# Second mixer of a two-layer backbone: queries and output projection with both parts of the rows side by side, two products a chunk for three

## The chip, the cores and the metric

The kernel is one program on one core of a Trainium2 chip. The metric is the device time of one execution in microseconds, the median of several runs. Five engines work side by side: TensorE (PE in the profile, with its weight loads as PEld), VectorE (DVE), ScalarE (ACT), GpSimd (POOL) and SyncE (SP), which issues nearly all DMA transfers. Each engine takes its own instructions strictly in an order that is fixed when the program is built; between engines there are semaphores only.

## The reference, cut to what matters

There are two layers over 256 latent and 256 context tokens of width 1024. The second layer's mixer is grouped-query attention, and since it is the last layer only the latent tokens get queries and an output:

```python
def odd_mixer(h_lat, h_ctx, w_in, w_out, qg, kg, cos, sin, need_ctx_out):
    q, k, v = split_cols(h_lat @ w_in, SIZES_ODD)           # 8 heads of 128; 2 key/value heads
    q = apply_rope(rms_norm(q.reshape(B, S, H_C, HD_C), qg), cos, sin) * HD_C ** -0.5
    k = apply_rope(rms_norm(k.reshape(B, S, KV_C, HD_C), kg), cos, sin)
    ...
    ck, cv = split_cols(h_ctx @ w_in[:, H_C * HD_C:], SIZES_ODD[1:])
    ...
    out_lat = block_attention(q, k_all, v_all) @ w_out
# in the layer loop
x_lat = x_lat + g1 * o_lat
h_lat = modulate(x_lat, norm_ffn_g[l], sh2, sc2)
y_lat = moe(h_lat, router_w, router_b, exp_w1[l], exp_w3[l], exp_w2[l])
```

## The kernel before, in words

Rows are kept transposed, features on the 128 partitions and tokens along the free axis (context in columns 0 to 255, latent tokens in 256 to 511). A projection by a 32-bit weight W of rows X is made on TensorE in a faster 32-bit format of fewer bits, so both operands are split into a high part and what is left of it, the low part: W = hi + lo, X = xhi + xlo. One chunk (128 of the 1024 input features) is then three products into the same accumulator, hi·xhi, lo·xhi and hi·xlo, made by `mm3` (line 1356; the products stand in the profile under line 1358). Weights are split by `splitw` (ScalarE casts hi at line 286, VectorE subtracts to get lo at line 287; two buffers of each).

The second mixer begins at line 1761 and goes through these stages, given by the order in which the code at its end issues them. An engine's instructions are put in order when the program is built, and products of neighbouring stages are mixed where the earlier ones would wait.

- `normed(m)` (lines 1784 to 1787) makes the high and the low part of the normalised rows, for latent tokens (m = 1) and then for context tokens (m = 0), for each of 8 chunks j: VectorE multiplies, ScalarE writes `h_hi[j]`, GpSimd makes the full value, VectorE subtracts to write `h_lo[j]`. These are the tiles g_hi and g_lo of the trace.
- `heads` (line 1821) with `head` (1798) makes the queries of heads 0 to 3 and the keys of the two key heads; later, between the attention of heads 0 to 3, the queries of heads 4 to 7. A head of queries is 8 chunks of three products over 256 columns; a head of keys is over all 512. `head` then squares the accumulator on ScalarE (1805) and scales it on VectorE into q1 or k1 (1806). `turn` (1809), issued one head later, sums the squares on TensorE (1812), rotates (1815 to 1819).
- `values` makes v; it and the keys are not touched by the change.
- `attend(h)` (1866 to 1889): scores (1871), softmax (1875 to 1879), transposes (1882, 1883), product with v (1886); ScalarE writes the high part of the result, `o_hi[h]` (1888), VectorE the low part `o_lo` (1889). `o_hi` takes over the buffers of q1.
- `out_half1(k0)` (1893) is the output projection, in two halves of four heads (k0 = 0 and 4); each makes 8 groups of 128 output features (2 weight tiles, m = 0 to 3 in each), a group being 4 chunks of three products over 256 columns. Then `residual` (1680, VectorE, 1684) adds gate times the accumulator to the residual stream XT. The first half is mixed with the attention of heads 4 to 7 and with products for the conditioning vectors (`bg`, line 261). The second half is mixed with `step(j)` of the expert front: square on ScalarE (341), scaling on VectorE (348), sums on TensorE (235).
- After it come the router and the experts of layer 1, whose weights stream through a ring of 1 MB buffers; a transfer is issued when a product has freed a buffer.

PSUM accumulators have tags with few buffers: "a", "t" and "o" have two each, "pj" and "ad" one.

Of the kernel before, what the change touches and what calls it, by code (L numbers as in the profile page):

```python
# [16 lines left out]
P = 128  # L17
# [66 lines left out]
def _model(tc, nc, ctx, A, out, dbg):  # L84
# [9 lines left out]
    def pt_(shape, tag, dt=F32):  # L94

        return psum.tile(shape, dt, tag=tag, name=tag, bufs=PB[tag])
# [1677 lines left out]
    A1, B1 = affine(1, 0, "mix")  # L1774
    h_hi = [hp.tile([P, T], F32R, name=f"g_hi{j}") for j in range(J)]
    h_lo = [hp.tile([P, T], F32R, name=f"g_lo{j}") for j in range(J)]

# [11 lines left out]

    q1 = [c1.tile([P, S], F32, tag="q1", name="q1", bufs=H_C) for _ in range(H_C)]  # L1790
    k1 = c1.tile([P, KV_C, T], F32, name="k1")
    v1 = c1.tile([P, NB, KV_C * HD_C], F32, name="v1")
    o_hi = {}
    o_lo = c1.tile([P, H_C, S], F32R, name="o_lo")
    rq1 = c1.tile([P, H_C, 2], F32, name="rq1")
    rk1 = c1.tile([P, KV_C, NB], F32, name="rk1")

    def head(hi, lo, dst, g, t0, tag):

        n = T - t0  # L1800
        ps = pt_([P, n], tag)
        for k in range(J):
            mm3(ps, hi[:, k, :], lo[:, k, :], h_hi[k][:, t0:], h_lo[k][:, t0:], k == 0, k == J - 1)
        sq = wt_([P, T], "y")[:, 0:n]
        SC.activation(sq, ps, AF.Square)
        V.tensor_scalar(dst, ps, g, None, op0=OP.mult)
        return sq
# [58 lines left out]
    def attend(h):  # L1866
# [18 lines left out]
        for c in range(NB):  # L1885
            PE.matmul(o, lhsT=v1[:, c, kv * P:(kv + 1) * P], rhs=pT[:, c, :], start=(c == 0), stop=(c == NB - 1))  # L1886
        o_hi[h] = c1.tile([P, S], F32R, tag="q1", name="o_hi", bufs=H_C)
        SC.copy(o_hi[h], o)
        V.tensor_tensor(o_lo[:, h, :], o, o_hi[h].bitcast(F32), op=OP.subtract)

    w_out1 = A["odd_w_out"][0].rearrange("(j p) c -> p j c", p=P)

    def out_half1(k0):
        for c in range(2):
            w = wtile(w_out1[:, k0:k0 + 4, c * 512:(c + 1) * 512], 4, 512)
            for m in range(4):
                hi, lo = splitw(w[:, :, m * P:(m + 1) * P])
                ps = pt_([P, S], ("pj", "o")[m % 2] if k0 else "pj")
                for k in range(4):
                    mm3(ps, hi[:, k, :], lo[:, k, :], o_hi[k0 + k], o_lo[:, k0 + k, :], k == 0, k == 3)  # L1900
                residual(c * 4 + m, ps, 2, 1, 1)
                yield
# [125 lines left out]
```

## Time and profile before

| | us |
|---|---|
| median of 3 runs | 1099.69 (1099.27 to 1100.06) |
| profiled execution, its own time | 1100.19 |
| span from its first to its last instruction | 1098.3 |
| TensorE busy | 984.2 (90%) |
| VectorE busy | 559.7 (51%) |
| ScalarE busy | 399.6 (36%) |

The second mixer lies at about 690 to 844 us of the span. In the profile L1358 is line 1358 of the kernel; a row of a group gives the busy time, the mean length of one and the idle time of the engine before it with what ended it. A timeline row gives start, length, engine, line, operation, output and inputs, shapes, and in brackets the idle time before and its releaser. Matmuls are pipelined: the start of one is recorded, its end is modelled, so the price of one in a stream is read from start to start.

### The profile page before, as it was taken

What the parts mean: (1) busy time and instruction counts of PE and PEld (TensorE: products, weight loads), DVE (VectorE), ACT (ScalarE), POOL (GpSimd) and SP (SyncE); (2) the same over time, 40 slices, a digit from 0 to 9 for tenths busy, and PEclk for the clock granted to TensorE, in tenths of its full rate; (3) what the DMA queues carried; (4) which work ended last, traced back from release to release, by engine and by line L of the source; (5) the groups of instructions that cost most, each with busy time, mean ns of one, the idle gap of its engine ahead of it and who ended that gap; (6) DMA issues with size and microseconds to landing.
All of it is one profiled execution on the core that took longest, in us unless ns stands there. A gap on an engine that the chain in (4) does not pass through costs nothing.

```text
span 1098.3 us, 14558 instructions
## 1 busy us (share of the span) xinstructions
PE 984.2 (90%) x5327; PEld 616.7 (56%) x5327; DVE 559.7 (51%) x1333; ACT 399.6 (36%) x735; POOL 91.1 (8%) x87
## 2 busy tenths in 40 slices
PE   5799999999999559999899999799998899988865
PEld 1577845556776357565566545468766454433322
DVE  3543389645877659575465623745766621101101
ACT  2532254437445227464535533324344121111100
POOL 0300000002000301211120100410100100000000
PEclk9899999999999769999989999899999799999988
DMA  9932237492328519999999999560198599999993
GB/s 376 300 123 83 77 146 256 168 340 77 123 109 322 215 56 361 388 392 395 401 404 383 409 401 371 201 232 2 61 357 348 205 419 420 420 419 420 421 419 113
DMA packets 71580, 305.70 MB, mean 278 GB/s; under 512 B 6096, under 2 KB 27856, under 8 KB 41168
## 3 DMA queue, kind: packets, MB, share of 16 engines
q1 hardware_dynamic: 61904, 290.23, 66.8%
q0 software_dynamic: 3072, 11.01, 3.8%
q10 hardware_dynamic: 6528, 3.47, 1.1%
q8 instruction: 44, 0.72, 0.3%
q14 instruction: 32, 0.26, 0.1%
HBM read 293.16 MB, written 11.53 MB: 277 GB/s over the span
## 4 chain that ended last, share of the span: by engine, by line
PE 30%; DMA 14%; DVE 4%; ACT 1%; issue 1%; POOL 0%; SPq 0%; DVEq 0%; ACTq 0%; POOLq 0%
DMA w<-in_exp_w_dram 13%; PE o L1011 5%; PE pj L1358 4%; PE o L235 3%; PE o L1050 2%; PE o L1886 1%; PE t L1358 1%; PE pj L998 1%; PE a L1871 1%; PE a L261 1%; PE o L1358 1%; DVE lo L287 1%; DMA xg<-rows,idx 1%; PE ad L261 1%; PE t L1882 1%; PE t L681 1%
## 5 line engine op out<-in xcount | busy, mean ns | idle before, releaser
L287 DVE TENSOR_TENSOR lo<-w,hi 128x1024 fp32r<-128x1024 f32 (+2 forms) x170 | 179.6, 1077 | 52.2 <-ACT hi L286 45.7
L286 ACT CAST hi<-w 128x1024 fp32r<-128x1024 f32 (+2 forms) x172 | 156.7, 928 | 111.0 <-PE o L1358 37.8
L1011 PE MATMUL o<-w,x 128*64 128x512 f32 x280 | 67.8, 596 | 0.0
L1028 DVE TENSOR_TENSOR ac<-ac,o 64x512 f32<-64x512 f32 x13 | 9.0, 691 | 110.5 <-ACT ac L1027 110.5
L702 PE MATMUL o<-lo,xh 128*128 128x512 f32 x128 | 51.8, 404 | 6.8 <-DVE lo L287 6.8
L681 PE MATMUL o<-w,xh 128*64 128x512 f32 x128 | 56.2, 595 | 0.1
L683 PE MATMUL o<-w,xh 128*64 128x512 f32 x128 | 56.2, 594 | 0.0
L261 PE MATMUL ad<-w,sl 128*32 128x512 f32 x320 | 50.8, 614 | 3.2 <-DMA w<-in_ada_w_dram 3.1
L701 PE MATMUL o<-hi,xh 128*128 128x512 f32 x128 | 51.6, 403 | 2.2 <-ACT hi L286 1.7
L703 PE MATMUL o<-hi,xl 128*128 128x512 f32 x128 | 50.9, 398 | 0.9 <-DVE xl L652 0.9
L1358 PE MATMUL pj<-h_hi,hi 128*128 128x512 f32 x104 | 43.8, 421 | 5.0 <-ACT h_hi L1345 2.6
L1027 ACT ACTIVATE ac<-o 64x512 f32<-64x512 f32 x13 | 7.7, 590 | 107.9 <-PE o L1011 63.2
L1358 PE MATMUL pj<-h_hi,lo 128*128 128x512 f32 x104 | 43.4, 418 | 0.2 <-DVE lo L287 0.2
L1358 PE MATMUL pj<-h_lo,hi 128*128 128x512 f32 x104 | 43.4, 417 | 0.0
L1011 PEld LDWEIGHTS o<-w,x 128*64 128x64 f32 x280 | 20.6, 137 | 37.9 <-issue 36.6
L235 PE MATMUL o<-w,x 128*32 128x512 f32 x256 | 31.4, 637 | 7.6 <-DMA w<-in_exp_w_dram 7.6
L681 PEld LDWEIGHTS o<-w,xh 128*64 128x64 f32 x128 | 17.0, 137 | 34.6 <-issue 33.4
L710 DVE TENSOR_TENSOR ac<-ac,o 128x512 f32<-128x512 f32 x12 | 8.2, 684 | 49.7 <-PE o L683 46.1
L1050 PE MATMUL o<-w,at 128*64 128x512 f32 x120 | 33.0, 597 | 0.0
L702 PEld LDWEIGHTS o<-lo,xh 128*128 128x128 f32 x128 | 24.6, 192 | 14.5 <-DVE lo L287 9.7
L1081 DVE SCALAR_TENSOR_TENSOR yl<-o,we,yh 128x512 fp32r<-128x512 f32 x12 | 8.9, 750 | 40.9 <-ACT yh L1080 40.9
L701 PEld LDWEIGHTS o<-hi,xh 128*128 128x128 f32 x128 | 24.5, 191 | 9.3 <-ACT hi L286 3.5
(589 smaller groups left out, 2269.4 us busy)
## 6 DMA issues: line engine op xcount, KB each, us to landing
w<-in_exp_w_dram SPq DMA_DIRECT2D x190, 1024.0 KB, 18.4
w<-in_ada_w_dram SPq DMA_DIRECT2D x48, 1024.0 KB, 6.7
w<-in_even_w_in_dram SPq DMA_DIRECT2D x12, 1024.0 KB, 12.1
w<-in_odd_w_in_dram SPq DMA_DIRECT2D x6, 1024.0 KB, 12.6
XT<-in_xT_dram SPq DMA_DIRECT2D x2, 2048.0 KB, 8.3
w<-in_even_w_out_dram SPq DMA_DIRECT2D x4, 1024.0 KB, 7.8
w<-in_odd_w_out_dram SPq DMA_DIRECT2D x4, 1024.0 KB, 9.0
yacc<-jp ACTq DMA_DIRECT2D x5, 512.0 KB, 9.7
```

Source lines behind the costliest of these rows:

```text
L235: done = PE.matmul(out[32 * q:32 * q + 32, :], lhsT=lhsT, rhs=rhs, start=start, stop=stop)
L261: PE.matmul(ps[32 * q:32 * q + 32, :], lhsT=sl[:, k, :], rhs=w[:, 0, q * 512:(q + 1) * 512], start=(k == 0), stop=(k == J - 1))
L286: SC.copy(hi, w)
L287: eng.tensor_tensor(lo, w, hi.bitcast(F32), op=OP.subtract)
L681: with_last = PE.matmul(out[HALF:], lhsT=lhsT[:, HALF:], rhs=rhs[1], start=start, stop=stop)
L683: PE.matmul(out[0:HALF], lhsT=lhsT[:, 0:HALF], rhs=rhs[0], start=start, stop=stop)
L701: PE.matmul(h_, lhsT=XH[i][:, k, :], rhs=hi[:, k % 2, :], start=(k == 0), stop=False)
L702: PE.matmul(h_, lhsT=XH[i][:, k, :], rhs=lo[:, k % 2, :], start=False, stop=False)
L703: PE.matmul(h_, lhsT=XL[i][:, k, :], rhs=hi[:, k % 2, :], start=False, stop=(k == J - 1))
L1011: PE.matmul(h[64 * c:64 * c + 64, :], lhsT=x[:, k, :], rhs=ws[c][:, i, :], start=(k == 0), stop=(k == J - 1))
L1050: PE.matmul(y[c][64 * i:64 * i + 64, :], lhsT=a[:, k, :], rhs=row_of(ws[q, i], k % 2)[:, c * 512:(c + 1) * 512], start=(k == 0), stop=(k = ...
L1358: f = (lambda a, b, **k: PE.matmul(ps, lhsT=b, rhs=a, **k)) if flip else (lambda a, b, **k: PE.matmul(ps, lhsT=a, rhs=b, **k))
```

## The change

The rows' two parts are put into one tile with an axis of two: `h2[j]` holds xhi and xlo of chunk j, `o2[h]` holds the two parts of an attention result (in the buffers of q1, which become twice as long; `o_lo` goes). A new `mm2` makes a chunk in two products: hi against both parts at once, 512 columns into an accumulator of two halves (hi·xhi and hi·xlo), and lo against xhi, 256 columns, into the first half. The two halves are then added: in `head` for queries by a ScalarE copy of the second half and a VectorE addition, in `out_half1` by calling `residual` once for each half. Keys keep three products of 512 columns, values keep theirs.

```diff
-    h_hi = [hp.tile([P, T], F32R, name=f"g_hi{j}") for j in range(J)]
-    h_lo = [hp.tile([P, T], F32R, name=f"g_lo{j}") for j in range(J)]
+    h2 = [hp.tile([P, 2, T], F32R, name=f"g{j}") for j in range(J)]
+    h_hi, h_lo = ([t[:, i] for t in h2] for i in range(2))
...
-    q1 = [c1.tile([P, S], F32, tag="q1", name="q1", bufs=H_C) for _ in range(H_C)]
+    q1 = [c1.tile([P, 2, S], F32, tag="q1", name="q1", bufs=H_C)[:, 0] for _ in range(H_C)]
...
-    o_hi = {}
-    o_lo = c1.tile([P, H_C, S], F32R, name="o_lo")
+    o2 = {}
...
+    def mm2(ps, hi, lo, x2, first, last):
+
+        PE.matmul(ps, lhsT=hi, rhs=x2, start=first, stop=False, skip_group_check=True)
+        PE.matmul(ps[:, 0], lhsT=lo, rhs=x2[:, 0], start=False, stop=last, skip_group_check=True)
+
     def head(hi, lo, dst, g, t0, tag):
 
         n = T - t0
+        sq = wt_([P, T], "y")[:, 0:n]
+        if t0:
+            ps = pt_([P, 2, n], tag)
+            for k in range(J):
+                mm2(ps, hi[:, k, :], lo[:, k, :], h2[k][:, :, t0:], k == 0, k == J - 1)
+            x = wt_([P, n], "sq")
+            SC.copy(x, ps[:, 1])
+            V.tensor_tensor(x, ps[:, 0], x, op=OP.add)
+            SC.activation(sq, x, AF.Square)
+            V.tensor_scalar(dst, x, g, None, op0=OP.mult)
+            return sq
         ps = pt_([P, n], tag)
         for k in range(J):
-            mm3(ps, hi[:, k, :], lo[:, k, :], h_hi[k][:, t0:], h_lo[k][:, t0:], k == 0, k == J - 1)
-        sq = wt_([P, T], "y")[:, 0:n]
+            mm3(ps, hi[:, k, :], lo[:, k, :], h_hi[k], h_lo[k], k == 0, k == J - 1)
...
-        o_hi[h] = c1.tile([P, S], F32R, tag="q1", name="o_hi", bufs=H_C)
-        SC.copy(o_hi[h], o)
-        V.tensor_tensor(o_lo[:, h, :], o, o_hi[h].bitcast(F32), op=OP.subtract)
+        o2[h] = c1.tile([P, 2, S], F32R, tag="q1", name="o2", bufs=H_C)
+        SC.copy(o2[h][:, 0], o)
+        V.tensor_tensor(o2[h][:, 1], o, o2[h][:, 0].bitcast(F32), op=OP.subtract)
...
-                ps = pt_([P, S], ("pj", "o")[m % 2] if k0 else "pj")
+                ps = pt_([P, 2, S], ("pj", "o")[m % 2] if k0 else "pj")
                 for k in range(4):
-                    mm3(ps, hi[:, k, :], lo[:, k, :], o_hi[k0 + k], o_lo[:, k0 + k, :], k == 0, k == 3)
-                residual(c * 4 + m, ps, 2, 1, 1)
+                    mm2(ps, hi[:, k, :], lo[:, k, :], o2[k0 + k], k == 0, k == 3)
+                for i in range(2):
+                    residual(c * 4 + m, ps[:, i], 2, 1, 1)
```

## Rows read from the trace of the kernel before

**Rows 1.** The page, part 2: the span in 40 slices of 27.5 us, in tenths.

```profile
PEclk9899999999999769999989999899999799999988
DMA  9932237492328519999999999560198599999993
```

**Rows 2.** Busy time by stretch: us, then engine by engine, granted clock, DMA share, GB/s.

```profile
702.00:740.00 38.00, 36.91 (x232) 25.27 (x230) 18.88 (x40) 11.53 (x18) 8.85 (x11) 1.00 0.69 249
752.00:788.00 36.00, 35.32 (x215) 28.69 (x213) 23.39 (x56) 18.45 (x38) 2.19 (x3) 1.00 0.00 1
788.00:827.00 39.00, 38.76 (x244) 25.25 (x243) 26.23 (x74) 16.05 (x33) 0.75 (x1) 1.00 0.85 330
827.00:844.00 17.00, 16.59 (x137) 13.81 (x136) 10.28 (x23) 7.60 (x16) 0.34 (x2) 1.00 1.01 415
```

**Rows 3.** Waits of TensorE, 690 to 850 us: total us, times, longest.

```profile
PE a L200 <- DVE rs L195: 4.6, 1, 4.6
...
PE ad L1812 <- ACT y L1805: 0.7, 1, 0.7
```

**Rows 4.** Timeline of TensorE in head 1: first and last of 17 products.

```profile
705.77 0.28 PE L1358 MATMUL pj<-g_hi,lo 128*128 128x256 f32 x1
...
707.64 0.28 PE L1358 MATMUL pj<-g_lo,hi 128*128 128x256 f32 x1
```

**Rows 5.** The same in a head of keys: first and last of 23 products.

```profile
732.34 0.39 PE L1358 MATMUL pj<-g_hi,lo 128*128 128x512 f32 x1
...
737.47 0.39 PE L1358 MATMUL pj<-g_lo,hi 128*128 128x512 f32 x1
```

**Rows 6.** Line 1358: weight loads, ns minimum/median/maximum.

```profile
L1358 PEld LDWEIGHTS pj<-g_hi,hi x56: 186/188/330, 694.9 to 785.5; 128*128 128x128 f32 x56
```

**Rows 7.** Chain of waits, first expert: 64 products of 512 columns.

```profile
867.31 13.88 PE o L1011 x64
```

**Rows 8.** Groups of VectorE, 690 to 850 us: busy us, mean ns.

```profile
L1684 DVE SCALAR_TENSOR_TENSOR XT<-pj,mod,XT 128x256 f32<-128x256 f32 x12 | 5.8, 483 | 7.0 <-PE pj L1358 6.8
L1817 DVE TENSOR_TENSOR sq<-o,cs 128x256 f32<-128x256 f32 x10 | 4.2, 416 | 0.0
...
L1806 DVE TENSOR_SCALAR q<-pj,qg 128x256 f32<-128x256 f32 x6 | 2.9, 480 | 4.2 <-ACT y L1805 4.2
```

**Rows 9.** Groups of ScalarE, 690 to 850 us.

```profile
L1805 ACT ACTIVATE y<-pj 128x256 f32<-128x256 f32 x6 | 2.3, 383 | 6.6 <-PE pj L1358 6.5
...
L1864 ACT COPY v<-o 128x256 f32<-128x256 f32 x2 | 0.7, 372 | 0.0
```

**Rows 10.** Timeline, start of the queries: first product, first low part of the rows.

```profile
693.73 0.58 PE L1358 MATMUL t<-g_hi,hi 128*128 128x256 f32 x1 [1.15 <-ACT g_hi L1785]
693.76 0.46 DVE L1787 TENSOR_TENSOR g_lo<-x,g_hi 128x256 fp32r<-128x256 f32 x1 [0.39 <-POOL x L1786]
```

**Rows 11.** Timeline of VectorE: the low part of the fourth context chunk.

```profile
712.97 0.43 DVE L1787 TENSOR_TENSOR g_lo<-x,g_hi 128x256 fp32r<-128x256 f32 x1
```

**Rows 12.** Timeline, end of head 7: its square, its sums on TensorE.

```profile
786.22 0.38 ACT L1805 ACTIVATE y<-pj 128x256 f32<-128x256 f32 x1 [1.79 <-PE pj L1358]
...
787.25 0.50 PE L1812 MATMUL ad<-ones,y 128*128 128x1 f32 x4
```

**Rows 13.** Timeline, attention of head 7: an addition, and the product with v.

```profile
822.47 0.48 DVE L1684 SCALAR_TENSOR_TENSOR XT<-pj,mod,XT 128x256 f32<-128x256 f32 x1
...
825.05 1.99 PE L1886 MATMUL o<-pT,v 128*128 128x256 f32 x8
```

**Rows 14.** Timeline, second half of the output: one group's round, and the last addition.

```profile
834.32 0.48 DVE L1684 SCALAR_TENSOR_TENSOR XT<-pj,mod,XT 128x256 f32<-128x256 f32 x1 [0.77 <-PE pj L1358]
...
835.11 0.69 DVE L287 TENSOR_TENSOR lo<-w,hi 128x512 fp32r<-128x512 f32 x1
...
836.29 0.28 PE L1358 MATMUL pj<-o_hi,hi 128*128 128x256 f32 x1
...
843.64 0.48 DVE L1684 SCALAR_TENSOR_TENSOR XT<-o,mod,XT 128x256 f32<-128x256 f32 x1 [1.30 <-PE o L1358]
```

## The prediction

> **What bounds the kernel now.** I read the page's slices first, then busy time by stretch, then TensorE's waits, then the timeline where the change falls. The mixer is slices 26 to 31 of the span; the granted clock there is at its upper level, 2.4 GHz, but for a dip in the first of them [rows 1]. In the four stretches from 702 to 844 us TensorE is busy 36.91 of 38.00, 35.32 of 36.00, 38.76 of 39.00 and 16.59 of 17.00 us [rows 2]. That is no proof, since matmul ends are modelled, but its waits agree: in 690 to 850 us the longest is the 4.6 us on the norms before the queries start, the next ones are under 1.2 us, and 0.7 us is typical [rows 3]. So the mixer is bound by TensorE's stream of products. VectorE is second: 26.23 of 39.00 us beside the attention of heads 4 to 7, and 10.28 of 17.00 us in the second output half [rows 2]. What the mixer loses or gains reaches the end one for one: transfers are nearly idle in slices 28 and 29, half idle in slice 32, and full in the seven slices after that [rows 1], so the experts' weights wait in a full ring until the first expert frees buffers, and from there they stream without a pause. A mixer that ends later shifts that stream as a whole.
>
> **The products.** The change touches 8 heads x 8 chunks and 16 groups x 4 chunks: 128 chunks, each from three products of 256 columns to one of 512 and one of 256. In a stream, 17 products of 256 columns start between 705.77 and 707.64: 1.87 / 16 = 116.9 ns each [rows 4]. 23 products of 512 columns start between 732.34 and 737.47: 5.13 / 22 = 233.2 ns each [rows 5]. A chunk goes from 3 x 116.9 = 350.7 ns to 233.2 + 116.9 = 350.1 ns. The columns are the same 768, and the price follows the columns: if each product had a fixed part a, then a = 2 x 116.9 - 233.2 = 0.6 ns. The gain is 128 x 0.6 ns = 0.08 us, taken as 0.1. Mixed widths in turn do not occur in the trace. The dearest the 512 can be I put at one more fixed part of 10 ns (it has two runs of 256), 1.3 us in all; the cheapest rate of 512 columns in the trace is 13.88 / 64 = 216.9 ns [rows 7], which is 16.3 ns less, 2.1 us in all. That one has weights of half the width, so I take the rows of this very line.
>
> One weight load in three goes as well. Its record is 188 ns long [rows 6], longer than the 116.9 ns from product to product, so loads already run under the products before them; a fixed part of 0.6 ns is all they leave open. The Trainium skill speaks otherwise on the page "TensorE: Matmul & The Clock Gate": section "Measured speedup vs the span model" says that a weight load overlaps with running products only when it goes to other row groups, and section "LDWEIGHTS (loading the stationary operand)" prices 128 columns at 128 / 1.2 = 107 ns. By these the dropped loads would give 128 x 107 ns = 13.7 us, an estimate from that page; the trace does not bear it out, since 116.9 ns cannot hold 256 columns and an open load of that size.
>
> **What is added.** Per head of queries: one ScalarE copy of 256 from PSUM, 0.37 us [rows 9], and one VectorE addition with a PSUM operand, 0.42 us [rows 8]; square and scaling stay at 0.38 and at most 0.48 us [rows 8, 9]. Per group of the output: a second addition of 0.48 us [rows 8]. In all 8 x 0.37 = 3.0 us on ScalarE and 8 x 0.42 + 16 x 0.48 = 11.0 us on VectorE. None of it is on TensorE, so it costs only where TensorE has nothing else to do. The accumulator is held as long as before: copy and addition, 0.37 + 0.42, stand for square and scaling, 0.38 + 0.48. The square is a new wait: ScalarE waits there for VectorE's addition, and behind it stands the cast of the weights of the head after next, which TensorE wants only after a whole head of products, 24 x 0.117 = 2.8 us, later. Place by place:
>
> - Start. The first product now reads the low part too. Before, it started at 693.73, while the first low part was ready at 693.76 + 0.46 = 694.22 [rows 10]. TensorE starts about 0.5 us later, but is paced by the norms there in any case, and its last chunk waits for the last low part before and after. Between 0 and 0.5; I take 0.2 us.
> - Heads 0 to 6: the longer way to the square is covered by the next head's 2.8 us. 0.
> - Head 7 has no head after it. Its square started at 786.22, its sums at 787.25 [rows 12]. Copy, addition and square with some 0.04 us between them end at 786.22 + 0.37 + 0.42 + 0.38 + 0.1 = 787.5. 0.2 us, unless output products go first (0).
> - Attention of heads 4 to 7 with the first output half: 8 additions of 0.48 us come into 39 us in which VectorE has 12.8 us free [rows 2]. Output products and conditioning products fill TensorE's gaps. 0 to 1.0; I take 0.5 us.
> - Head 7's attention has the fewest fillers left. The addition at 822.47 lies ahead of its last scaling, and the product with v starts at 825.05 [rows 13]; a second addition pushes it by up to 0.5 us. I take 0.4 us.
> - Second output half. After a group's products VectorE does addition and scaling (834.32 to 835.11, 0.79 us) and the low weights of the group after next, ready at 835.80, while TensorE needs them about 0.12 us after 836.29 [rows 14]. The slack is 0.6 us here, where sums stand between the groups, and some 0.5 us less where none do. A second addition takes 0.5 us of it: 0 to 0.4 us for each of three such pairs. I take 0.2 us in all.
> - The end. After the last group nothing is left to cover: the addition at 843.64 [rows 14] is followed by a second that has to wait for it, then scaling, sums and the router. 0.5 us, certain.
>
> Sum: 0.2 + 0.2 + 0.5 + 0.4 + 0.2 + 0.5 - 0.1 = 1.9 us. I take 0.2 off, since an order made with the new operations in view can put products into the two gaps that have some: 1.7 us. The profiled execution goes from 1100.19 (span 1098.3, 1.9 outside it) to 1101.9; the median is 0.5 below it, so from 1099.69 to 1101.4.
>
> **Rivals.**
>
> A. All of it is hidden but the end. VectorE has 12.8 us free beside attention and 6.7 us in the second half [rows 2], which speaks for it; that it is already the next to finish in a round [rows 14] speaks against. 0.5 - 0.1: 1100.1 us.
>
> B. Slower by more: VectorE becomes the bound of an output group. A group then has two additions at 0.52, scaling 0.27 and low weights 0.62 (starts one after another) = 1.93 us on VectorE, against 12 x 0.117 = 1.40 plus 0.28 us for its share of the sums on TensorE, 1.69. It decides from the point at which VectorE has 1.69 us in a group; then each of 16 groups costs 0.24 us, 3.8 us, and with head 7 and the end 4.5 us: 1104.2. Only the second half is near that point. Of this kind also is that the change does not do what it says: if the read of both parts, which spans the context's columns of the low part, were made to wait for them, head 1 (products from 705.77 [rows 4]) would wait for the fourth context chunk, ready at 712.97 + 0.43 [rows 11]. With conditioning products in the gap that is some 4 us: 1103.7.
>
> C. Faster: 512 columns at the cheapest rate of the trace, 16.3 ns less [rows 5, 7], with most of the additions hidden: -2.1 + 0.4 = 1098.0. Against it: all products of this line keep to their columns.
>
> D. Faster by far: a weight load lies open. At the length of its record [rows 6] that would be 128 x 188 ns = 24 us, 1075.6. The spacing of rows 4 and 5 leaves 0.6 ns for it. The rule of the Trainium skill named above, page "TensorE: Matmul & The Clock Gate", is of this kind; by its price the time would be 1086.
>
> **How the numbers follow.** Forecast 63%, A 8%, B 17%, C 10%, D 2%. A measurement of this kernel can tell about 0.2%, 2.2 us, from no change: from 1097.5 to 1101.9. The forecast's own terms run from 0.6 (only start, end and products at their low ends) to 3.2 us, around 1.7, so of its 63% I put 39 within 0.2% and 24 above. Same: 39 + 8 = 47%. Slower: 24 + 17 = 41%. Faster: 10 + 2 = 12%. The range goes from C's 1098.0 to a little above B's 1104.2, 1104.8; D, half of C and the mixtures of B's two kinds lie outside it.
>
> **What would show it.** In the profile after: the first product of a chunk should start 233 ns before the second and that 117 ns before the next chunk, else the products are mispriced. 64 products fewer stand in each of the two places, and as many weight loads. TensorE's waits in the mixer should be longer by 1 to 2 us in all: on the low part at the start, on ScalarE's square of head 7, on the product with v of head 7, and on VectorE in the second half. VectorE's idle time before the additions of the second half should fall from 0.7 us to nearly none; if it falls to none and TensorE waits for low weights in every group, B holds. The router's first operation should come 1 to 2 us later, and the last transfers by as much. The prediction is wrong if a chunk is not at 350 ns, or if the order of products is so changed that the start of the queries or the hand-over to the attention of head 4 moves by microseconds.

## The result, and the profile after

The changed kernel takes 1106.79 us (median; 1106.50 to 1108.26), the kernel before in the same session 1099.88: a ratio of 1.0065, 95% interval [1.0038, 1.0093]. It is slower by 6.9 us; forecast were 1101.4, with a range up to 1104.8. The profiled execution took 1108.26 (span 1106.5), against 1100.19 (span 1098.3).

First the page's slices after (span in 40 slices of 27.7 us), to be laid beside [rows 1]:

```profile
PEclk9899999999999679999999999899999799999988
DMA  9932246482428429999999999540386499999993
```

The picture is the same: the clock dips in nearly the same slices, transfers are nearly idle in the same slice of the mixer and full in the last ones. So the loss lies inside the mixer. Busy time by stretch after (columns as in [rows 2]; the stretches are the first output half with the attention of heads 4 to 7, and the second output half with its end):

```profile
787.60:830.60 43.00, 40.66 (x210) 23.50 (x209) 28.56 (x78) 16.42 (x34) 0.74 (x1) 1.00 0.83 324
830.60:853.40 22.80, 20.05 (x118) 13.13 (x118) 14.64 (x34) 8.04 (x16) 0.45 (x2) 1.00 0.78 311
```

The same two stretches of the kernel before:

```profile
787.90:827.20 39.30, 39.06 (x245) 25.54 (x244) 26.33 (x74) 16.18 (x34) 0.75 (x1) 1.00 0.85 329
827.20:845.30 18.10, 17.70 (x147) 14.28 (x146) 10.77 (x25) 7.90 (x17) 0.45 (x2) 1.00 0.99 401
```

These two stretches are called C and D from here on. C begins with the first output product; D begins with the first product of the second half that goes into accumulator o (or t), and ends where VectorE's copy of the finished sums (y<-a) starts. C grew from 39.3 to 43.0 us, D from 18.1 to 22.8: 8.4 us. Of these TensorE is idle for 4.5 us more (0.64 before, 5.09 after) and busy for 4.0 us more, although its columns are the same: 1.8 of that is conditioning (below), the rest lies in many small pieces. D's 4.7 us are 1.7 up to the start of its second group (3.1 us before, 4.8 after), 1.6 from there to the start of the last group's first addition (13.3 and 14.9) and 1.4 at the end (below).

The stages ahead of C gained 2.1 us: from the first product with rs to the first 512-column product of the second head of keys 40.56 us before and 39.27 after, from the first scores to the first output product 35.02 and 34.26. The rest is not the change: the mixer's start is 1.7 us later (rs at 691.47 and 693.18), in code that the change doesn't touch (in the kernels below that start lies between 689.9 and 695.6), and from the end of D to the end of the span it is 252.98 before and 253.09 after (below between 249.5 and 255.6, and 262.7 in e9, in code that is the same everywhere). So outside C and D single profiles differ by microseconds, and a kernel's C + D and its median need not agree to better than 1 or 2 us. Here -2.1 + 8.4 + 1.7 + 0.1 = 8.1 of the profiled 8.2 us.

TensorE's waits after, 690 to 854 us (total us, times, longest), beside [rows 3]:

```profile
PE t L1799 <- DVE g L1787: 1.8, 1, 1.8
PE o L376 <- DVE XT L1684: 1.0, 1, 1.0
PE ad L1826 <- ACT y L1819: 0.7, 1, 0.7
PE pj L1799 <- DVE XT L1684: 0.7, 2, 0.6
PE pj L1799 <- DVE A1ffn L275: 0.7, 1, 0.7
PE pj L321 <- ACT brow L318: 0.7, 1, 0.7
PE o L1799 <- ACT hi L286: 0.6, 1, 0.6
PE t L368 <- DVE y L365: 0.5, 1, 0.5
PE o L1800 <- DVE lo L287: 0.5, 2, 0.2
```

In C and D the waits on the additions (XT), on high and on low weights are new, and so are two of 0.7 us on what is made from the conditioning products (A1ffn, brow). There the kernel before waited 0.4 us on lgb and 0.2 us on mx and for nothing else. How such waits arise can be seen in one group of the second half, first TensorE, then VectorE:

```profile
835.83 0.40 PE L1799 MATMUL pj<-o,hi 128*128 128x512 f32 x1
836.06 0.28 PE L1800 MATMUL pj<-o,lo 128*128 128x256 f32 x1
836.18 0.40 PE L1799 MATMUL pj<-o,hi 128*128 128x512 f32 x1
...
838.36 0.38 PE L1800 MATMUL o<-o,lo 128*128 128x256 f32 x1 [0.23 <-DVE lo L287]
...
838.93 0.40 PE L1799 MATMUL pj<-o,hi 128*128 128x512 f32 x1
```

```profile
837.08 0.48 DVE L1684 SCALAR_TENSOR_TENSOR XT<-pj,mod,XT 128x256 f32<-128x256 f32 x1 [1.50 <-PE pj L1800]
837.61 0.69 DVE L287 TENSOR_TENSOR lo<-w,hi 128x512 fp32r<-128x512 f32 x1
838.22 0.48 DVE L1684 SCALAR_TENSOR_TENSOR XT<-pj,mod,XT 128x256 f32<-128x256 f32 x1
838.74 0.35 DVE L348 TENSOR_SCALAR u<-XT,A1ffn 128x256 f32<-128x256 f32 x1
```

A chunk costs 0.23 + 0.12 us, as forecast. But the two additions of a group don't follow each other: VectorE does low weights between them, so that the only "pj" accumulator is free at 838.70 instead of 837.56. Here nobody waits for that, since the next product into pj follows the group in o at 838.93; what TensorE waits for is the low weights behind the first addition, 0.23 us. The second addition in turn pushes the scaling u, and so the sums. The stage's end, from both engines:

```profile
849.99 0.28 PE L1800 MATMUL o<-o,lo 128*128 128x256 f32 x1
850.11 0.38 PE L376 MATMUL o<-ident,u 128*128 128x128 f32 x2
851.46 0.52 PE L376 MATMUL o<-ident,u 128*128 128x128 f32 x3 [0.97 <-DVE XT L1684]
```

```profile
850.31 1.00 DVE L1684 SCALAR_TENSOR_TENSOR XT<-o,mod,XT 128x256 f32<-128x256 f32 x2 [0.72 <-PE o L1800]
...
853.41 0.42 DVE L365 COPY y<-a 128x256 f32<-128x256 f32 x1 [1.69 <-PE a L235]
```

From the start of the last addition(s) to the copy of the sums it is 850.31 to 853.41, 3.1 us; before it was 843.64 [rows 14] to 845.32, 1.7 us. Before, transposes of u filled TensorE from 843.44 to 844.57, beside the last addition; in the new order two of them are left there (850.11), TensorE waits 0.97 us, and the other transposes and the sums follow. That makes 1.4 us instead of the 0.5 us forecast.

### The profile page after: what moved, and what is told of

The parts are those of the page before. It is cut to its first block, busy times and chain, and to the rows that moved or that the text cites. A ratio compares the mean times of both kernels' runs of the same rounds, so it can differ in the third digit from the quotient of the medians.

```text
span 1106.5 us, 14343 instructions
## 1 busy us (share of the span) xinstructions
PE 988.4 (89%) x5199; PEld 611.4 (55%) x5199; DVE 568.5 (51%) x1357; ACT 402.4 (36%) x743; POOL 93.2 (8%) x87
## 4 chain that ended last, share of the span: by engine, by line
PE 40%; DVE 5%; DMA 3%; ACT 2%; issue 1%; POOL 0%; DVEq 0%; ACTq 0%; POOLq 0%
PE o L1011 6%; PE o L235 4%; PE o L681 2%; PE o L1050 2%; PE pj L1799 2%; DMA w<-in_exp_w_dram 2%; PE o L1900 1%; PE a L1885 1%; PE o L702 1%; PE t L681 1%; PE pj L998 1%; PE o L703 1%; PE pj L1800 1%; PE o L701 1%; DVE lo L287 1%; PE a L261 1%
## 5 line engine op out<-in xcount | busy, mean ns | idle before, releaser
L1684 DVE SCALAR_TENSOR_TENSOR XT<-pj,mod,XT 128x256 f32<-128x256 f32 x58 | 26.7, 480 | 14.5 <-PE pj L1358 7.9
L1081 DVE SCALAR_TENSOR_TENSOR yl<-o,we,yh 128x512 fp32r<-128x512 f32 x12 | 8.9, 750 | 42.3 <-ACT yh L1080 42.3
```

## The experiments

Theories, numbered as the expectations name them. **1**: the accumulator is held longer, since two operations read it. **2**: VectorE's work as such. **3**: the products, of mixed widths, are dearer than they look. **4**: TensorE's order, which is made anew when the kernel is built, becomes worse with the added operations (conditioning products in more pieces, sums and transposes where they wait). **5**: VectorE's own order: an operation added in it delays what stands behind.

All runs, with C and D of their profiles in us (before: 39.3, 18.1; changed kernel: 43.0, 22.8); each ratio is to the kernel before as it ran beside that run (medians 1099.13 to 1099.93):

| run | what is made | median us | ratio to before, 95% | C | D |
|---|---|---|---|---|---|
| e1_queries_only | change, output as before | 1097.97 | 0.9983 [0.9970, 0.9995] | 39.3 | 18.1 |
| e2_output_only | change, queries as before | 1109.06 | 1.0094 [1.0079, 1.0108] | 44.4 | 21.2 |
| e8_second_half_only | change, first output half as before | 1103.64 | 1.0036 [1.0020, 1.0052] | 39.3 | 21.2 |
| e3_more_accumulators | change, accumulators pj, t, o, t in the second half | 1105.25 | 1.0055 [1.0041, 1.0069] | 43.0 | 21.8 |
| e4_additions_in_a_row | change, low weights queued behind both additions | 1104.62 | 1.0055 [1.0037, 1.0073] | 42.3 | 22.7 |
| e5_second_read | before + second VectorE operation, reads accumulator | 1106.53 | 1.0067 [1.0050, 1.0085] | 43.4 | 20.3 |
| e6_second_operation_no_read | before + the same without that read | 1103.93 | 1.0044 [1.0027, 1.0060] | 42.8 | 20.2 |
| e7_second_half_by_gpsimd | change, second half by ScalarE and GpSimd | 1107.48 | 1.0074 [1.0055, 1.0094] | 42.8 | 23.9 |
| e9_conditioning_split | before, conditioning asked for later | 1114.73 | 1.0132 [1.0104, 1.0160] | 43.9 | 19.9 |
| e13_conditioning_in_one | e9 + more accumulators | 1122.47 | 1.0232 [1.0199, 1.0265] | 55.2 | 19.7 |
| e11_second_read_unsplit | e13 + second read | 1125.48 | 1.0244 [1.0215, 1.0274] | 56.4 | 22.4 |
| e12_change_unsplit | e13's edits on the change | 1125.40 | 1.0247 [1.0221, 1.0273] | 57.2 | 22.6 |
| e14_order_of_e5_alone | before, in TensorE's order of e5 | 1105.06 | 1.0045 [1.0030, 1.0061] | 43.3 | 19.7 |
| e15_e5_in_order_of_before | e5, in TensorE's order of before | 1107.01 | 1.0069 [1.0053, 1.0085] | 42.2 | 21.2 |
| e16_change_in_order_of_before | change, in that order | 1107.12 | 1.0070 [1.0053, 1.0088] | 44.6 | 22.3 |
| e17_vector_time_only | that order, VectorE operation nobody waits for | 1102.86 | 1.0029 [1.0018, 1.0039] | 40.9 | 19.3 |
| e18_second_read_by_scalar | that order, accumulator copied by ScalarE | 1104.46 | 1.0043 [1.0027, 1.0059] | 42.6 | 19.8 |
| e19_e6_in_order_of_before | e6, in that order | 1102.95 | 1.0030 [1.0018, 1.0041] | 40.9 | 20.6 |

**Which part loses.** e1 makes the output with three products again and one addition (the diff), e8 only its first half (the same for k0 = 0); e2 makes the queries with three products (the branch for t0 in `head` is dropped).

```diff
-                    mm2(ps, hi[:, k, :], lo[:, k, :], o2[k0 + k], k == 0, k == 3)
-                for i in range(2):
-                    residual(c * 4 + m, ps[:, i], 2, 1, 1)
+                    mm3(ps, hi[:, k, :], lo[:, k, :], o2[k0 + k][:, 0], o2[k0 + k][:, 1], k == 0, k == 3)
+                residual(c * 4 + m, ps, 2, 1, 1)
```

> The change is kept for the queries (two products a chunk, ScalarE copy and VectorE addition) and undone for the output projection (three products of 256, one addition a group). Theory 1 (accumulator held: in the output projection VectorE squeezes the weights' subtraction between the two additions of a group, so the one pj accumulator comes free over 1 us later and TensorE waits) and theory 2 (VectorE's additional work itself bounds the output groups) both put the whole loss into the output: this kernel is then not slower than the kernel before, 1098 to 1100 us, since in the profile after the two query stretches are 1.3 and 0.8 us shorter than before. Theory 3 (a 512 beside a 256 product costs more in some way the spacing doesn't show): half of the loss stays, about 1103 us.

> The change is kept for the output projection and undone for the queries. Theories 1 and 2: the whole loss stays, and what the query stretches gained is gone, 1107 to 1109 us. Theory 3: about 1103 us. If the parts are independent, this kernel's loss and the one of the queries alone add up to the 6.9 us of the whole change.

> The change for the queries and for the second half of the output projection; the first half, which is mixed with attention and conditioning products, has three products and one addition again. By the stretches of the profile after, the first half lost 3.7 us and the second 4.7 us: theories 1 and 2 give 1098 + 4.7, about 1102.5 us. If instead the loss is a chance of one order of products, it is not divided so: anything from 1098 to 1107 us.

The queries' part alone is faster than both kernels: 1097.97 us, 0.17% below before, and its C and D are those of before. The output's part loses all of it, C + D 65.6 us for 57.4. The halves do not simply add up: with the second alone C is as before and D 3.1 us longer, where the whole change has 3.7 and 4.7 us. So 1.6 us of D's loss come only with the first half changed.

**Hold, VectorE's work, or the products.** e3 gives the second half more accumulators, e4 queues the low weights behind both additions of the group two before (`added` lists each group's second addition):

```diff
-                ps = pt_([P, 2, S], ("pj", "o")[m % 2] if k0 else "pj")
+                ps = pt_([P, 2, S], ("pj", "t", "o", "t")[m] if k0 else "pj")
...
-                hi, lo = splitw(w[:, :, m * P:(m + 1) * P])
+                with tc.issue_after(added[-2].ins) if len(added) > 1 else ExitStack():
+                    hi, lo = splitw(w[:, :, m * P:(m + 1) * P])
```

e5 puts a second VectorE operation on the kernel before, with its old products, after each `residual` (`zero1` is 0, so the rows stay as they are); e6 reads `cs[:, 0, :]`, a table in SBUF, in place of the accumulator. e7 takes VectorE's second addition from the change:

```diff
+                V.scalar_tensor_tensor(XT[:, c * 4 + m, L:], ps, zero1, XT[:, c * 4 + m, L:], op0=OP.mult, op1=OP.add)
```

```diff
-                for i in range(2):
-                    residual(c * 4 + m, ps[:, i], 2, 1, 1)
+                x, j = wt_([P, S], "sq"), c * 4 + m
+                SC.activation(x, ps[:, 1], AF.Copy, scale=mod[1][:, 2, j, 1:2])
+                residual(j, ps[:, 0], 2, 1, 1)
+                GP.tensor_tensor(XT[:, j, L:], XT[:, j, L:], x, op=OP.add)
```

> The whole change, but the second half of the output projection goes round four accumulators (pj, t, o, t) instead of two (pj, o). Theory 1: a held accumulator hurts less, the second half gets 3 us or more back of its 6, about 1103 us. Theory 2: VectorE has the same work, so nothing changes, 1106 to 1107 us.

> The whole change, but VectorE's subtraction for the weights of the group after next is queued behind both additions of a group, so that the second addition follows the first at once and frees the accumulator about 0.6 us earlier; the work is the same. Theory 1: most of the second half's 6 us comes back, about 1102 us. Theory 2: VectorE's work is the same and the weights come later, so the time stays or rises, 1106.5 to 1108 us.

> The kernel before, all products as they were, with a second VectorE operation behind each addition of the output projection that adds the accumulator times zero: the same engine, length, source and order as the second addition of the change, and the accumulator is held until it is done. Theory 1 (the accumulator is held) and theory 2 (VectorE's added work) both give what the output's part of the change costs by the run of the output alone, 7 to 10 us, 1106 to 1109 us: then products and their widths have no part in it. Theory 3 (the two widths cost TensorE more): 1099 to 1101 us.

> As the run before it, but the second operation reads a table in SBUF times zero in place of the accumulator: VectorE has the same number of operations in the same chain, while the accumulator is free after the first. Theory 1: little is left, 1100 to 1102.5 us, mainly the last addition at the end. Theory 2: the same loss as with the second read, 1106 to 1109 us.

> The whole change, but the output's second half is scaled out of PSUM by ScalarE (a copy of 256) and added in SBUF by GpSimd, so VectorE has one addition a group as before; the accumulator is held by ScalarE's copy and then by VectorE's addition, together about as long as by two additions. Theory 2: VectorE's load is that of before, so the output's loss goes and the gain of the queries stays, 1098 to 1100.5 us. Theory 1: the accumulator is still held, most of the loss stays, 1103 to 1107 us.

e5 has the old products and loses 7 us: theory 3 falls. Relieving the accumulators of the second half gives back about 1 us (ratios of 1.0055 for 1.0065, and 64.8 and 64.9 us in C + D for 65.8), no more than the intervals can tell; the first half's one accumulator is as it was. In e4 all additions of the second half stand in a row and D is 22.7 us for 22.8, so the low weights between them are not what D loses by. Without the read (e6) 4.4 us of e5's loss are left, so theory 1 alone does not hold. Without VectorE's second addition (e7) all of the change's loss is left, but that says little against theory 2: in e7 VectorE's scaling waits for GpSimd's additions, 3.0 us in four waits, and C has kept 3.5 of its 3.7 us. Each kernel's order of TensorE was another, which led to theory 4.

**Conditioning in pieces.** In a trace a conditioning product (line 261, four side by side, 32 weight columns each) has two records. Timeline of TensorE, kernel before:

```profile
810.81 1.04 PE L261 MATMUL ad<-w,sl 128*32 128x512 f32 x2
811.79 1.14 PE L1882 MATMUL t<-ident,p 128*128 128x128 f32 x8
812.86 1.07 PE L261 MATMUL ad<-w,sl 128*32 128x512 f32 x8
813.85 1.99 PE L1886 MATMUL o<-pT,v 128*128 128x256 f32 x8
```

One product takes 0.98 us, four take 0.99. The changed kernel:

```profile
789.27 2.76 PE L261 MATMUL ad<-w,sl 128*32 128x512 f32 x18
791.96 0.50 PE L1799 MATMUL pj<-o,hi 128*128 128x512 f32 x1
...
793.56 1.06 PE L261 MATMUL ad<-w,sl 128*32 128x512 f32 x6
794.55 1.12 PE L1885 MATMUL a<-k,q 128*128 128x512 f32 x2
```

Nine take 2.69, three 0.99. The 32 products of C take 8.64 us in 7 pieces before, 10.46 in 8 after, 11.43 in 9 in e5, 10.74 in 10 in e6. To test this, e9 asks for them later, which changes the pieces without any added operation; e13 leaves 1 and 31 in a row, and e11 and e12 put the second read and the change on it. The first edit is in all four (conditioning steps asked for in the first output half), the second in all but e9:

```diff
-A1C=[2,1]*4
+A1C=[0]*8
...
-                ps = pt_([P, S], ("pj", "o")[m % 2] if k0 else "pj")
+                ps = pt_([P, S], ("pj", "t", "o", "t")[m] if k0 else ("pj", "ad")[m % 2])
```

> The kernel before, with the conditioning products no longer asked for between the output groups and the attention steps (A1C is all zero), so that they come after the first output half; nothing else is changed, no operation added or dropped. In TensorE's order they then stand in pieces of 5, 4, 4, 4, 4 and 11 products instead of 8, 4, 8, 4 and 8, so that every conditioning step (4 products side by side) but the last two is cut in two. Fourth theory (a cut step costs TensorE about 1 us whatever the size of the piece, and the added additions of the change lose their time by cutting steps and by waits): 13 pieces of 0.98 us instead of 9, so conditioning takes TensorE 12.5 us instead of 8.6, and the kernel takes about 1103.5 us, 1.0035 of before, without any new operation. Theories 1 and 2 (only the hold of the accumulator, only VectorE's work): nothing of theirs changes, 1099.5 to 1100.5 us.

> The kernel before, without conditioning products asked for between the output groups (A1C all zero) and with more accumulators for the output groups (pj and ad in turn in the first half; pj, t, o, t in the second). The conditioning products then stand in TensorE's order as 1 and 31 in a row. It is the base for the next two runs. Fourth theory: 9 pieces as before, so no loss from cuts; but the gaps of the last attention heads have fewer fillers, 0 to 2 us: 1099.5 to 1102. Theories 1 and 2 say nothing of it.

> The run before this one (conditioning in one, more accumulators) with the second VectorE operation for each output group of e5 (it reads the accumulator, times zero, and adds to the residual). There it cost 7 us. Here the conditioning products stand as 1 and 31 in a row with or without it, so no step can be cut by it, and a held accumulator blocks nobody in the next group. Fourth theory: what is left is the wait at the end, about 1 us, and some 0.5 to 1 us of waits: at most 2 us over the run of conditioning in one. Theory 1 (the hold of the accumulator): about 1 to 2 us too. Theory 2 (VectorE's work as such bounds the groups): 6 to 7 us over it, as in e5.

> The changed kernel with the same two edits (conditioning in one, more accumulators). Fourth theory: the queries' gain of about 2 us stays, the output part costs 1 to 2 us at the end and in waits instead of 8.4: 0 to 1 us below the run of conditioning in one, about 1099 to 1101.5. Theory 2: the output part still costs 7 to 8 us, so 5 to 6 us over that run, about 1105 to 1107.

My count for e9 was wrong: its pieces of 5, 4, 4, 4 and 4 products took 1.83, 0.99, 1.00, 1.00 and 0.99 us, though each four are three of one step and one of the next. The price goes by the four that start together, not by the step. Still C and D grew by 6.4 us with no operation added, but not by the order alone: the granted clock was 0.95 in C and 0.84 in D (before: 1.00), and TensorE waited 1.4 us for the transfer of conditioning's weights. The rest of e9's loss lies behind the mixer (from the end of D to the end of the span 262.7 us for 253.0) and wasn't followed up. The other three fell out of the question they were made for: conditioning now waits for the transfer of its weights, as TensorE's waits of e13 show (690 to 870 us):

```profile
PE ad L261 <- DMA w<-in_ada_w_dram: 8.5, 5, 3.4
```

This covers what else is lost in C. D is clear of it: 19.7 in e13, 22.4 in e11, 22.6 in e12, so the second operation costs 2.7 us in D with no conditioning near and four accumulators. The granted clock in D is 0.85, 0.89 and 0.88 there, so the difference holds for that lower clock only.

**The order held fixed.** The last six runs queue TensorE's instructions of C and D one behind the other in a given order, so that order and operations can be exchanged. e14 gives the kernel before the order of e5; e15 gives e5, and e16 the change, the order of before (`ORDER` lists the instructions of C and D as they stand in the other kernel):

```diff
+            for a, b in zip(ORDER, ORDER[1:]):
+                self.tc.add_manual_dep(self.done[b], self.done[a].name, mybir.DependencyInfo(mybir.DependencyClass.NoSync, mybir.DependencyReason.DATA), reason="order")
```

> The kernel before, operation for operation, with TensorE's instructions from the first output product to the end of the second half queued in exactly the order in which they stand in e5 (the kernel before with a second addition for each group); no second addition. Fourth theory in its present form (the added operations lose their time by the order of TensorE that is made with them: conditioning products in more pieces, sums and transposes in places where they wait): most of e5's loss of 7.0 us is there without the operations, 1103.5 to 1105.5 us. Theories 1 and 2 (the operations themselves: the accumulator held longer, VectorE's work): little of it, 1099.5 to 1101 us.

> e5 (a second addition for each output group), with TensorE's instructions in that stretch queued in the order in which they stand in the kernel before. Fourth theory: the loss shrinks from 7.0 us to what the waits cost, 1 to 2.5 us: 1100.5 to 1102 us. Theories 1 and 2: the loss stays or grows, since the products then wait where the order of e5 stepped round a held accumulator: 1106 us or more.

> The changed kernel with TensorE's instructions in that stretch queued in the order of the kernel in which only the queries are changed (which stands as in the kernel before there), the third product of each output chunk left out of the list. Fourth theory: the queries' gain of 2 us stays and the output part costs 1 to 3 us instead of 8.4: 1098.5 to 1101 us, no slower than the kernel before. Theories 1 and 2: 1106 us or more, as the change.

Busy time by stretch (C, then D) of e14 and of e15:

```profile
791.40:834.60 43.20, 42.03 (x245) 26.23 (x244) 26.35 (x74) 16.01 (x34) 0.75 (x1) 1.00 0.83 323
834.60:854.30 19.70, 19.04 (x149) 14.70 (x147) 10.85 (x26) 7.89 (x17) 0.45 (x2) 1.00 0.87 345
```

```profile
788.80:831.00 42.20, 39.79 (x246) 25.53 (x245) 29.07 (x82) 16.27 (x34) 0.75 (x1) 1.00 0.83 323
831.00:852.20 21.20, 18.87 (x149) 14.53 (x147) 14.06 (x33) 8.46 (x17) 0.45 (x2) 1.00 0.85 343
```

Theory 4 is half right, and not as the cause. The order of e5 costs 5.1 us (5.6 in C + D) with not one operation added: TensorE is busy 4.3 us longer and idle 1.2. But e5 in the old order loses as much as in its own: 7.1 us (6.0 in C + D), now mostly as idle time: 4.7 us, 0.6 before. So the operations are the cause. The order made for them hardly avoids any of the loss; it turns waits into conditioning pieces and other busy time. In e16 the change is no better in the old order either (66.9 us in C + D for 65.8).

**What an added operation does.** With the order of before held, one property at a time, each after `residual`: e17 adds VectorE's time alone (the first line; `cs[:, 1, :]` is no longer used there), e18 a second reader alone (the second line), e19 is e6, where the residual rows are finished later as well. Only TensorE's order is held: VectorE's and ScalarE's are made anew, and in e17 some of VectorE's other operations change places too. In these runs a product stands under line 115 and a transpose under 118, those of the helper that holds the order.

```diff
+                V.scalar_tensor_tensor(cs[:, 1, :], cs[:, 0, :], zero1, XT[:, c * 4 + m, L:], op0=OP.mult, op1=OP.add)
...
+                SC.copy(cs[:, 1, :], ps)
```

> The kernel before with TensorE's order of the stretch held as it is, and after each output group's addition a VectorE operation of the same size (0.48 us) that reads the residual and writes a table no longer used: it holds no accumulator and nobody waits for its result. What it can cost is VectorE's time alone: whatever stands behind it on VectorE (softmax of the last heads, low weights, scaling) comes up to 0.48 us later. Fifth theory (VectorE's fixed order is the path: an operation between an accumulator's addition and the softmax or low weights delays TensorE there, although VectorE has idle time elsewhere): 3 to 5 us, 1103 to 1105. First theory (the accumulator held by a second read): 0 to 1 us, 1099.5 to 1101.

> The kernel before with TensorE's order of the stretch held as it is, and for each output group a ScalarE copy of the accumulator into a table no longer used (0.37 us): the accumulator has a second reader, VectorE has nothing more to do, nobody waits for the result. Fifth theory: 0 to 2 us (ScalarE is at 16 of 39 us there, and its copy can lie beside VectorE's addition): 1099.5 to 1102. First theory (the accumulator held by a second read): 3 to 5 us, 1103 to 1105.

> e6 (a second VectorE operation on the residual after each group, reading no accumulator) with TensorE's order of the stretch held as in the kernel before. Against the run with VectorE's time only, the residual rows are now finished 0.5 us later, for which the scaling, the squares, the sums and the end of the stage wait; against e15 the accumulator is not held. Fifth theory: 1 to 1.5 us above the run with VectorE's time only, 0 to 1 us below e15: 1104.5 to 1106.5. First theory: 0 to 1.5 us above the kernel before.

e17 loses 2.9 us (2.8 in C + D) for operations whose result nobody waits for. TensorE's waits, 786 to 850 us, begin with

```profile
PE t L118 <- DVE p L1923: 1.0, 2, 0.8
```

How such a wait arises is seen in the smaller of the two, in the softmax of one head. VectorE, then TensorE beside it:

```profile
811.85 0.15 DVE L1922 RECIPROCAL sm<-sm 128x1 f32<-128x1 f32 x1
811.96 0.48 DVE L1948 SCALAR_TENSOR_TENSOR cs<-cs,zero,XT 128x256 f32<-128x256 f32 x1
812.36 0.48 DVE L1923 TENSOR_SCALAR p<-p,sm 128x512 f32<-128x512 f32 x1
```

```profile
812.17 0.65 PE L118 MATMUL t<-ident,p 128*128 128x128 f32 x4
812.99 0.63 PE L118 MATMUL t<-ident,p 128*128 128x128 f32 x4 [0.17 <-DVE p L1923]
```

The added operation (cs) stands ahead of the second scaling of p, and the four transposes behind that scaling wait. In the kernel before those eight transposes ran without a gap (811.79 above). VectorE is idle for 11.7 of the 40.9 us of this C, yet not at that place.

The hold by itself is e15 against e19: the order of TensorE is the same, the added operations are the same and equally long (0.48 us), only their source is the accumulator in e15 and a table in e19. e15 is slower by 4.1 us (the intervals of the two ratios lie apart), by 1.9 in C + D. TensorE's waits of e15, 786 to 853 us, have

```profile
PE pj L115 <- DVE XT L1948: 1.1, 2, 0.5
```

and two more on XT of 0.2 us each, as transposes too wait for these accumulators; in e19 no wait on XT is left.

e18 loses 4.5 us (5.0) for a second reader without any work for VectorE. But it is not the reader alone: the copies stand in ScalarE's queue. TensorE's waits of e18, 786 to 850 us, begin with

```profile
PE pj L115 <- ACT cs L1946: 1.9, 2, 1.4
```

The longer of the two lasts 1.43 us, up to 823.38, and is for the copy in the last row of ScalarE here:

```profile
821.57 1.28 ACT L1988 ACT_TABLE_LOAD   x1
822.87 0.20 ACT L1988 ACTIVATE nothing<-ones 128x1 f32<-128x1 f32 x1
822.97 0.35 ACT L1946 COPY cs<-pj 128x256 f32<-128x256 f32 x1
```

VectorE's addition of that group ended at 821.65; the copy stands behind the load of a table that ScalarE makes in the kernel before too (at 822.45), with no copy behind it. So this wait is theory 5 on ScalarE, and part of its loss is a follow-on, in the busy time of three stretches:

```profile
822.40:824.40 2.00, 1.02 (x6) 1.02 (x7) 0.99 (x2) 1.44 (x4) 0.00 (x0) 0.82 1.04 430
824.40:826.40 2.00, 2.00 (x11) 2.00 (x11) 0.17 (x1) 0.59 (x1) 0.00 (x0) 0.50 1.00 414
826.40:828.40 2.00, 2.00 (x10) 1.79 (x10) 1.18 (x2) 0.95 (x2) 0.00 (x0) 0.82 1.01 418
```

TensorE was busy for 1.02 of the 2.00 us of the first (the wait lies in it), and the granted clock went to 0.82 there and to 0.50, its lower level of 1.2 GHz, in the next. Counted by the granted clock that is 0.36 + 1.00 + 0.36 = 1.7 us of e18's loss. With the 1.4 us of the wait, 3.1 of the 5.0 us in C + D come from this one place in ScalarE's queue. e16's profile has the same fall (0.50 from 826.2 to 828.2 us); in C of the changed kernel the clock is 1.00.

So e15's loss of 7.1 us is, step by step and by the medians, VectorE's time 2.9 (e17), late rows 0.1 (e19 less e17) and the hold 4.1 (e15 less e19); in C + D of the profiles it is 2.8, 1.3 and 1.9 of 6.0. The late rows can't be told from nothing, and the 1 to 1.5 us that theory 5 gave them did not come in the medians. Theory 5 and theory 1 hold both, each for a part; theory 2 in the form of VectorE as the bound falls with its idle time.

What stays open: the change loses 8.4 us in C + D, e5 6.4. The 2 us between them were not taken apart, and the two parts were measured on the kernel before with operations added, not on the change itself. Nor was the mechanism of the queries' gain tried by itself; in the trace a conditioning piece fewer (10.77 us for 11.75 ahead of the second head of keys) is half of it.

## Why the prediction was wrong

- **What bounds the mixer** (TensorE's stream, and a loss passes on one for one): right. From the end of D to the end nothing changed (253.0 and 253.1).
- **The products**: right. 0.23 + 0.12 us a chunk against 350.1 ns; no fixed part, no cheaper 512. With a third of the weight loads of these products gone and nothing gained by it, rivals C and D are out. The Trainium skill, page "TensorE: Matmul & The Clock Gate", section "The mechanism" (the prediction names another section), lets a weight load overlap with running products only on other row groups. For loads of this shape this trace does not agree: the 13.7 us that the prediction estimated by it are nowhere.
- **Start and heads**: mis-sized, with the wrong sign in sum. The first product does come later by 0.6 us against rs (2.90 for 2.26; I had 0.5, taken as 0.2). But the stages ahead of the output gained 2.1 us where I had a loss of 0.4. The step that failed is that only the places with a new operation were priced, and the order around them taken as it stood; it was made anew, with a conditioning piece fewer (1.0 us). What the other 1.1 us are stays open.
- **Attention with the first half**: a step that failed. I took 0.5 of 0 to 1.0 and 0.4 for head 7's attention, 0.9 in all, because VectorE had 12.8 us free and "Output products and conditioning products fill TensorE's gaps". Measured: 3.7 us. Free time in sum said nothing of the place (e17). And the fillers are not free to fill: with the order made anew they became dearer by pieces (10.46 for 8.64 us), with the order of before held TensorE waits instead (e16: C is 44.6 us).
- **"The accumulator is held as long as before"** was said of the queries, and no price was put on the hold in the output, where the first half has one accumulator. That term was put at nothing; on the kernel before it measured 4.1 us by the medians and 1.9 in C + D (e15 less e19), beside 2.9 and 2.8 for VectorE's time (e17).
- **Second half and end**: 0.2 + 0.5 us; measured 4.7, the furthest off, of which 1.4 at the end. The slack of 0.6 us from [rows 14] was right for one group in the old order. I had put the low weights behind both additions and they went between them, but that is not the reason, since with them behind both D stays (e4). 1.6 of the 4.0 us missed come only with the first half changed (e8); the rest was not taken apart.
- **The take of 0.2 us off for an order made with the new operations in view** can't be told from nothing. With the operations, the order made for them gains 0.1 us on the old one (e5 against e15) and 0.3 (the change against e16); without them that of e5 costs 5.1 (e14).
- **The spread**: the bounds listed place by place add up to 0.4 to 3.8 us ahead of the 0.2 taken off, not to 0.6 to 3.2; 6.9 lies outside both.
- **Rival B** gave the side and two thirds of the size (4.5 of 6.9 us). As a bound VectorE shows only in part: it is idle for 8.2 of 22.8 us in D, but for only 0.9 us between 840.52 and 849.59, and there TensorE waits for it once, 0.18 us. B's 1.69 us a group for TensorE was too low: before, the additions from 832.07 to 843.64 stand 1.93 us apart on average. The false wait on the context's columns did not come: no such wait stands among TensorE's.

## What to carry to other kernels

An operation added to an engine with idle time is priced at its place in that engine's queue, by what stands behind it and who waits for that, and not by the idle time of the stretch. A product form that saves nothing on TensorE but needs a second reader for each accumulator can lose where accumulators are few, so measure the parts of such a change apart (the queries alone here: 0.9983, for a reason not shown; the output alone: 1.0094). Where the order of the bounding engine is made at build time, hold it fixed once to see whether a loss comes from the operations or from the new order. And a probe that moves work to another engine tests that engine's queue as well (the copies of e18 behind a table load).

## What the runs showed of the hardware

Conditioning products side by side on 32 weight columns cost 0.90 to 0.99 us for each four that start together (eight 1.86, nine 2.69), and the same for one or three alone (0.98, 0.99). A filler cut at the wrong place is paid as a whole one. And waits on TensorE can cost once more through its clock: where it was busy for 1.02 of 2.00 us, the granted clock fell to the lower level for about 3.4 us, 1.7 us of work at the upper one (e18); in C of the changed kernel, with 2.3 us idle in all, it stayed at 1.00.
